# One attention kernel's first three head pairs: dividing by the row sums in the output projection, two value blocks to a PSUM bank, and every block of the first pair split

## The chip, the cores and the metric

The kernel is one program on one core of a Trainium2 chip. Its time is the device time in microseconds (us). The engines are PE (TensorE, the matrix engine; its sequencer also loads weights, PEld), DVE (VectorE), ACT (ScalarE), POOL (GpSimd) and SP (SyncE, whose queue starts the DMAs here).

## What is computed

Two decoder layers run over 1024 tokens of width 1024. In each, one projection feeds four mixers; their outputs are concatenated, projected and normalised, and a gated feed-forward follows. The part that matters is the softmax attention of two mixers, each of four heads:

```python
def one_block(args):
    q_blk, start = args
    s = jnp.einsum('bqhd,bkhd->bhqk', q_blk, k).astype(jnp.float32) * scale
    q_pos = start + jnp.arange(BLOCK)
    s = jnp.where(key_pos[None, :] <= q_pos[:, None], s, -jnp.inf)
    p = jax.nn.softmax(s, axis=-1).astype(v.dtype)
    return jnp.einsum('bhqk,bkhd->bqhd', p, v)
...
y = jnp.concatenate([y_a, y_b, y_c, y_d], axis=-1) @ w_out[l]
x = _layer_norm(DEEPNORM_ALPHA * x + y, ln1_g[l], ln1_b[l])
```

`y_b` (latent attention) is of this form; `y_c` (dilated windows, merged by their denominators) is computed by the kernel as one masked softmax too. Row sums divide the products of `p` and `v`; dividing before or after the product with `v` is the same.

## The kernel before

A layer's stages follow each other: the mixers without softmax, the projections for the others, `attention` (L1083, about 280 to 444 us in layer 0 and 1478 to 1642 in layer 1), `out_proj` (L1179), and the feed-forward.

**Attention** takes four head pairs, G[0] to G[3]: the first two are the dilated mixer's (mask `maskC`), the last two the latent one's (`maskB`). `attn` (L800) makes 16 rows of each pair: two heads (hh) by eight query blocks (i = 2*jp + e) of 128 tokens, with jp taken as (0,3) and then (1,2). A row goes through these steps: scores on PE into `sc`; DVE adds the mask and takes the minimum (L824); ACT takes exp in place and adds the row up (L828); DVE takes the sum's reciprocal (L830); POOL multiplies the row by it (L831); PE transposes the row's key blocks (L848) into a bank `pt`; ACT writes their rounded high part PH (L146) and DVE the rest, PL (L149). After both rows of a jp, PE adds up the value products into `pv` (L875), once with PH and once with PL. V holds a high and a low part in 128 columns, so a block's result has two 64-row parts that are added later. The table `FULL` lets some jp of a pair go undivided into high and low: G[0]'s jp 0 and 1 are copied whole (L854, by turns on ACT and DVE) and multiplied once, in fp32, by 64 columns of V.

ACT evacuates `pv` (L886, or L883) into `tmp` of 256 columns. For G[0] to G[2] two DMAs (L889) spill its parts to `yp` in memory; for G[3] DVE adds the parts into `Yb` (L884).

PE's order is written by hand: scores run three rows ahead (`ahead`), value sums follow two rows behind (VLAG), and projections of the next pair are filled in between (`self.jobs`). The other engines' orders come from a scheduler. PSUM pools are `mm` (3 banks: value sums and projections), `s` (2: scores) and `t` (3: transposes).

**out_proj** works on halves h of the tokens. `ysplit` brings eight operands: g = 0 and 3 come whole (L1192); for g = 1 and 2 the spilled parts are loaded (L1199) into one of two buffers, added on DVE (L1202), then cast on ACT and their rest taken on DVE (g = 1) or POOL (L149). The operand for f = 1 of g = 1 is `Yb`. PE's products are `po` (L124); DVE adds them to x (L1218).

The tags that matter in the rows below: `sc`, `pt`, `pv`, `po` are PSUM banks, `P` a row, `mn` its minimum, `rs` its sum, `yr` a loaded part and `yT` an operand of the projection.

## Time and profile before

| | us |
|---|---|
| median of 3 runs | 2399.78 |
| lowest and highest | 2398.84, 2403.02 |
| the profiled execution | 2400.5 |
| its span, first to last instruction | 2398.8 |

The mean granted TensorE clock of the profiled execution was 0.996 of full speed. Durations in the text are this execution's. Of an engine's busy time only what the others wait for counts, and that is read in the stretch where it happens: the rows of a stretch give the busy time of each engine in it, the waits give what ended an engine's idle time, and a timeline lists instructions with their start.

### The profile page before, as it was taken

What the parts mean: (1) busy time and instruction counts of PE and PEld (TensorE: products, weight loads), DVE (VectorE), ACT (ScalarE), POOL (GpSimd) and SP (SyncE); (2) the same over time, 40 slices, a digit from 0 to 9 for tenths busy, and PEclk for the clock granted to TensorE, in tenths of its full rate; (3) what the DMA queues carried; (4) which work ended last, traced back from release to release, by engine and by line L of the source; (5) the groups of instructions that cost most, each with busy time, mean ns of one, the idle gap of its engine ahead of it and who ended that gap; (6) DMA issues with size and microseconds to landing.
All of it is one profiled execution on the core that took longest, in us unless ns stands there. A gap on an engine that the chain in (4) does not pass through costs nothing.

```text
span 2398.8 us, 33440 instructions
## 1 busy us (share of the span) xinstructions
PE 2346.0 (98%) x11804; PEld 1971.7 (82%) x11804; DVE 1612.9 (67%) x2925; ACT 1004.8 (42%) x2004; POOL 1176.9 (49%) x1097
## 2 busy tenths in 40 slices
PE   9999999999999999999999999999999999999998
PEld 9789878777888888888897898788778888888886
DVE  7743588478765566767957435784787665667689
ACT  6323578334332323544343225783343323235442
POOL 2223525373545455767622244253735455547676
PEclk9999999999999999999999999999999999999999
DMA  4201112522332324653222110135213333345521
GB/s 169 65 29 43 31 37 83 186 110 70 115 114 87 113 99 170 216 189 101 93 66 64 36 37 31 38 87 188 110 62 114 116 102 107 108 164 208 189 97 70
DMA packets 91446, 246.81 MB, mean 103 GB/s; under 512 B 12096, under 2 KB 18560, under 8 KB 91280
## 3 DMA queue, kind: packets, MB, share of 16 engines
q1 hardware_dynamic: 91280, 244.68, 30.1%
q8 instruction: 94, 1.54, 0.3%
q14 instruction: 72, 0.59, 0.1%
HBM read 180.64 MB, written 64.52 MB: 102 GB/s over the span
## 4 chain that ended last, share of the span: by engine, by line
PE 82%; DVE 9%; issue 3%; ACT 3%; POOL 2%; DMA 1%; SPq 0%; POOLq 0%; ACTq 0%; DVEq 0%
PE gu L124 34%; PE dn L124 14%; PE zc L124 6%; PE po L124 5%; PE zvo L572 4%; PE zdq L524 3%; PE za L124 3%; PE zb L124 3%; PE pv L875 2%; PE sc L124 2%; PE dl L124 2%; DVE P L824 1%; PE pt L848 1%; DVE x L1136 1%; DVE PL L149 1%
## 5 line engine op out<-in xcount | busy, mean ns | idle before, releaser
L124 PE MATMUL gu<-T,fc 128*128 128x512 f32 x2640 | 625.9, 395 | 5.1 <-DVE T L1374 5.1
L124 PEld LDWEIGHTS gu<-T,fc 128*128 128x128 f32 x2640 | 496.7, 188 | 123.3 <-DVE T L1374 6.6
L1279 POOL TENSOR_TENSOR fc<-fw,fc 128x512 fp32r<-128x512 f32 x232 | 325.5, 1406 | 348.8 <-ACT fc L1278 341.9
L124 PE MATMUL dn<-dc,dc 128*128 128x512 f32 x1512 | 352.2, 395 | 0.0
L124 PEld LDWEIGHTS dn<-dc,dc 128*128 128x128 f32 x1512 | 283.7, 188 | 68.3 <-DVE dc L1279 1.0
L1278 ACT CAST fc<-fw 128x512 fp32r<-128x512 f32 x232 | 142.8, 620 | 349.5 <-PE gu L124 218.5
L124 PE MATMUL gu<-B,fc 128*128 128x512 f32 x1056 | 260.0, 396 | 0.0
L124 PEld LDWEIGHTS gu<-B,fc 128*128 128x128 f32 x1056 | 197.6, 188 | 46.6
L149 POOL TENSOR_TENSOR dc<-hr,dc 128x512 fp32r<-128x512 f32 x126 | 190.1, 1520 | 79.4 <-ACT dc L146 69.9
L1437 DVE TENSOR_TENSOR Ra<-Ra,gu 128x512 f32<-128x512 f32 x172 | 117.6, 684 | 118.6 <-PE gu L124 101.8
L831 POOL TENSOR_SCALAR P<-P,rs 128x256 f32<-128x256 f32 (+7 forms) x128 | 95.8, 752 | 152.4 <-DVE rs L830 94.9
L124 PE MATMUL po<-wh,yT 128*128 128x512 f32 x512 | 163.2, 397 | 0.6 <-DVE x L1218 0.6
L124 PE MATMUL zc<-wh,xT 128*128 128x384 f32 x512 | 134.1, 339 | 0.0
L1278 ACT CAST dc<-dr 128x512 fp32r<-128x512 f32 x108 | 67.0, 622 | 129.9 <-PE dn L124 75.1
L124 PEld LDWEIGHTS po<-wh,yT 128*128 128x128 f32 x512 | 95.8, 188 | 23.4 <-DVE x L1218 1.5
L124 PE MATMUL sc<-kst,q 128*128 128x512 f32 (+3 forms) x384 | 107.7, 375 | 6.7 <-DVE mn L824 6.6
L828 ACT ACTIVATE P<-P,mn 128x256 f32<-128x256 f32 (+7 forms) x128 | 99.9, 782 | 21.4 <-DVE mn L824 19.8
L1279 DVE TENSOR_TENSOR dc<-dr,dc 128x512 fp32r<-128x512 f32 x72 | 81.1, 1136 | 35.4 <-ACT dc L1278 35.4
L149 DVE TENSOR_TENSOR PL<-pt,PH 128x512 fp32r<-128x512 f32 (+3 forms) x176 | 95.6, 557 | 12.3 <-ACT PH L146 11.8
L140 POOL TENSOR_TENSOR wl<-raw,wh 128x768 fp32r<-128x768 f32 (+2 forms) x32 | 62.6, 1962 | 79.6 <-ACT wh L132 79.1
L124 PE MATMUL po<-wl,yT 128*128 128x512 f32 x256 | 100.7, 395 | 0.0
L848 PE MATMUL pt<-ident,P 128*128 128x128 f32 x576 | 89.2, 281 | 11.4 <-DVE PL L149 5.7
(393 smaller groups left out, 4896.3 us busy)
## 6 DMA issues: line engine op xcount, KB each, us to landing
fw<-in_wGU SPq DMA_DIRECT2D x88, 512.0 KB, 4.6
hr<-hs SPq DMA_DIRECT2D x142, 256.0 KB, 2.8
dr<-in_wD SPq DMA_DIRECT2D x44, 512.0 KB, 5.2
hs<-Ra SPq DMA_DIRECT2D x40, 512.0 KB, 2.9
hs<-Rb SPq DMA_DIRECT2D x22, 512.0 KB, 5.5
raw<-in_wO SPq DMA_DIRECT2D x16, 512.0 KB, 3.6
x<-x SPq DMA_DIRECT2D x16, 512.0 KB, 2.6
raw<-in_wC SPq DMA_DIRECT2D x16, 384.0 KB, 3.0
```

What stands on the lines that cost most here:

```text
L124: self.nc.tensor.matmul(out, lhsT=a, rhs=b, start=first and j == 0, stop=last and j == n - 1)
L140: (eng or nc.gpsimd).tensor_sub(lo[:, :n], raw[:, :n], f32(hi[:, :n]))
L149: (lo_eng or nc.vector).tensor_sub(lo, src, f32(hi))
L524: step(lambda: nc.tensor.matmul(pz, lhsT=a, rhs=b_, start=n == 0, stop=n == 23))
L572: nc.tensor.matmul(box["p"], lhsT=a, rhs=b_, start=j == 0, stop=j == 23)
L828: nc.scalar.activation(P[:, 0:nk], P[:, 0:nk], AF.Exp, scale=-1.0, bias=m, accum_out=rs[:, 0:1])
L831: nc.gpsimd.tensor_scalar(out=P[:, 0:nk], in0=P[:, 0:nk], scalar1=rs[:, 1:2], scalar2=1.0, op0=ALU.mult, op1=ALU.mult)
L848: nc.tensor.transpose(pt[:, b * 128:(b + 1) * 128], P[:, (b0 + b) * 128:(b0 + b + 1) * 128], self.ident)
L875: nc.tensor.matmul(pv[0:m, c0:256], lhsT=v(b), rhs=Pt[b // 4][:, b % 4, c0:256], start=b == 0 and x == 0, stop=b == nb - 1 and x == len(pa ...
L1278: nc.scalar.copy(dst[:, 0:512], src)
L1279: lo_eng.tensor_sub(dst[:, 512:1024], src, f32(dst[:, 0:512]))
L1437: tt = lambda o, a, b, op: v.tensor_tensor(out=o, in0=a, in1=b, op=op)
```

## The change

In G[0] to G[2], exp adds each row's sum into a column of a tile `sums` (128 x 16), and neither reciprocal nor multiplication follows. When a pair is through, `turn_sums` takes the reciprocal of the whole tile, turns it on PE, copies it on ACT and writes it to `yr` in memory. In `out_proj` two DMAs load these factors, each row spread over 64 partitions, into `rb`, and POOL multiplies the added spilled parts by them. G[3] still divides its rows. FULL is now empty, so all blocks of G[0] are split. And the two jp that follow each other (0 and 3, 1 and 2) put their sums into the halves of one bank, which is evacuated once, 512 columns at a time, and spilled by half as many DMAs.

```diff
@@ -34,7 +34,7 @@
 LATE_Y = 6
 SEQ, VLAG = "svt", 2
 AHEADS = (3, 3, 3, 3)
-FULL = [("AV",) * n + ("",) * (4 - n) for n in (2, 0, 0, 0)]
+FULL = [("AV",) * n + ("",) * (4 - n) for n in (0, 0, 0, 0)]
 NLAG, MAN = 0, {mybir.EngineType.PE}
 PPS = ("E", "B", "B", "B")
 NP = NF // 2
@@ -802,7 +802,7 @@
         nc = self.nc
 
         rows = [(G, jp, hh, 2 * jp + e) for G in groups for two in ((0, 3), (1, 2)) for hh in range(2) for e in range(2) for jp in two]
-        P_, PHL, norms = {}, {}, []
+        P_, PHL, norms, open_pv = {}, {}, [], [None]
 
         def scores(n):
             G, jp, hh, i = rows[n]
@@ -824,6 +824,11 @@
                 nc.vector.tensor_tensor_reduce(out=P[:, k0:k1], in0=sp[:, 0:k1 - k0], in1=mask[:, m0:m0 + k1 - k0], scale=-scale,
                                                scalar=mn[:, ch - 1:ch] if ch else 3.0e38, op0=ALU.add, op1=ALU.min, accum_out=mn[:, ch:ch + 1])
             m = mn[:, nch - 1:nch]
+            if "sums" in G:
+
+                c = hh * 8 + i
+                nc.scalar.activation(P[:, 0:nk], P[:, 0:nk], AF.Exp, scale=-1.0, bias=m, accum_out=G["sums"][:, c:c + 1])
+                return
             rs = self.sm("rs", 2)
             nc.scalar.activation(P[:, 0:nk], P[:, 0:nk], AF.Exp, scale=-1.0, bias=m, accum_out=rs[:, 0:1])
             def norm():
@@ -860,7 +865,15 @@
             V = G["V"]
             full = G["full"][jp]
             nb = 2 * jp + 2
-            pv = self.psum("pv", "mm")
+
+            both = not any(G["full"])
+            if both:
+                second = jp >= 2
+                if not second:
+                    open_pv[0] = self.psum("pv", "mm")
+                pv = open_pv[0][:, 256 * second:256 * second + 256]
+            else:
+                pv = self.psum("pv", "mm")
             pairs = PHL.pop((id(G), jp, hh))
             if "heads" in G:
                 v = lambda b: V[b // 2][:, b % 2, G["heads"] + hh, :]
@@ -874,15 +887,24 @@
                 for x, Pt in enumerate(pairs):
                     nc.tensor.matmul(pv[0:m, c0:256], lhsT=v(b), rhs=Pt[b // 4][:, b % 4, c0:256],
                                      start=b == 0 and x == 0, stop=b == nb - 1 and x == len(pairs) - 1)
+            if both:
+                if not second:
+                    return
+                pv, tmp = open_pv[0], self.t2("tmp")
+                blocks = lambda x: x.rearrange("p (j n) -> p j n", n=256)
+                if jp == 3:
+                    at = lambda x: blocks(x)[:, 0:4:3, :]
+                else:
+                    at = lambda x: blocks(x)[:, 1:3, :]
+                if "Y" in G:
+                    nc.scalar.copy(tmp[0:64, :], pv[0:64, :])
+                    nc.vector.tensor_tensor(out=at(G["Y"][64 * hh:64 * hh + 64, :]), in0=blocks(tmp[0:64, :]), in1=blocks(pv[64:128, :]), op=ALU.add)
+                    return
+                nc.scalar.copy(tmp, pv)
+                for part in range(2):
+                    nc.sync.dma_start(at(G["spill"][part][64 * hh:64 * hh + 64, :]), blocks(tmp[64 * part:64 * part + 64, :]))
+                return
             tmp = self.t2("tmp", 256)
-            if "Y" in G:
-                y = G["Y"][64 * hh:64 * hh + 64, jp * 256:(jp + 1) * 256]
-                if full:
-                    nc.scalar.copy(y, pv[0:64, 0:256])
-                else:
-                    nc.scalar.copy(tmp[0:64, :], pv[0:64, 0:256])
-                    nc.vector.tensor_tensor(out=y, in0=tmp[0:64, :], in1=pv[64:128, 0:256], op=ALU.add)
-                return
             nc.scalar.copy(tmp[0:m, :], pv[0:m, 0:256])
             for part in range(2):
                 dst = G["spill"][part][64 * hh:64 * hh + 64, jp * 256:(jp + 1) * 256]
@@ -1093,17 +1115,33 @@
                     zjobs.pop(0)()
         box = {}
 
+        def sums(g):
+            G[g]["sums"] = self.sp.tile([128, 16], F32, name=self.nm("sums"), tag="sums", bufs=2)
+
+        def turn_sums(g):
+
+            t = G[g]["sums"]
+            nc.vector.reciprocal(t, t)
+            pt = self.psum("prs", "t")
+            nc.tensor.transpose(pt[0:16, 0:128], t, self.ident)
+            r = self.t2("rsT", 128)
+            nc.scalar.copy(r[0:16, :], pt[0:16, 0:128])
+            nc.sync.dma_start(io["yr"][l, g], r[0:16, :])
+
         def start0():
+            sums(0)
             G[0].update(mask=self.mask, spill=io["yp"][l, 0])
             self.jobs = zjobs + self.prep_c_jobs(zc[1], G[1])
 
         def start1():
+            sums(1)
             G[1].update(mask=G[0]["mask"], spill=io["yp"][l, 1])
             w = box["w"] = self.b_weights(l)
 
             def st():
                 bb["qk"] = self.qk_tiles("E", G[0]["qk"][2])
             self.jobs = self.b_vqr_jobs(ct, w, bb) + [st] + self.b_qk_jobs(0, ct, w, bb, "qk")
+            self.jobs.insert(4, lambda: turn_sums(0))
 
         def start2():
             m = self.u("maskB")
@@ -1111,10 +1149,13 @@
             box["Yb"] = self.u("Yb", F32, "A")
             bb["qk1"] = self.qk_tiles("A", G[1]["qk"][2])
             G[2].update(heads=0, mask=m, spill=io["yp"][l, 2], qk=bb["qk"], V=bb["V"], R=bb["R"], QR=bb["QR"][0])
+            sums(2)
             self.jobs = self.b_qk_jobs(1, ct, box["w"], bb, "qk1")
+            self.jobs.insert(2, lambda: turn_sums(1))
 
         def start3():
             G[3].update(heads=2, mask=G[2]["mask"], Y=box["Yb"], qk=bb["qk1"], V=bb["V"], R=bb["R"], QR=bb["QR"][1])
+            self.jobs = [lambda: None, lambda: None, lambda: turn_sums(2)]
 
         for g, f in zip(G, (start0, start1, start2, start3)):
             g["start"] = f
@@ -1198,8 +1239,13 @@
                         raw = self.uw("yr", F32, "r")
                         nc.sync.dma_start(raw[:, 0:1024].rearrange("p (a n) -> p a n", a=2),
                                           io["yp"][l, f if g == 2 else 2][:, :, h * 512:h * 512 + 512].rearrange("a p n -> p a n"))
+                        gg = f if g == 2 else 2
+                        rb = self.t2("rb")
+                        for hh in range(2):
+                            nc.sync.dma_start(rb[hh * 64:hh * 64 + 64, :], io["yr"][l, gg].rearrange("(a t) p -> a (t p)", a=2)[hh:hh + 1, h * 512:(h + 1) * 512].to_broadcast([64, 512]))
                         y[f] = raw[:, 0:512]
                         nc.vector.tensor_tensor(out=y[f], in0=y[f], in1=raw[:, 512:1024], op=ALU.add)
+                        nc.gpsimd.tensor_tensor(out=y[f], in0=y[f], in1=rb, op=ALU.mult)
                 for f in range(2):
                     k = g * 2 + f
                     t = self.u("yT", F32R, "y" if g == 1 and h == 1 else "A").rearrange("p (a n) -> p a n", a=2)
@@ -1771,6 +1817,7 @@
     io["crow"] = nc.dram_tensor("crow", (L, 8, 512), F32, kind="Internal").ap()
     io["ys"] = nc.dram_tensor("ys", (L, 2, 2, 128, 1024), F32, kind="Internal").ap()
     io["yp"] = nc.dram_tensor("yp", (L, 3, 2, 128, 1024), F32, kind="Internal").ap()
+    io["yr"] = nc.dram_tensor("yr", (L, 3, 16, 128), F32, kind="Internal").ap()
     io["x1"] = nc.dram_tensor("x1", (L, S, D), F32, kind="Internal").ap()
     io["hs"] = nc.dram_tensor("hs", (L, NP, 4, 128, S), F32, kind="Internal").ap()
     io["xs"] = nc.dram_tensor("xs", (S, D), F32, kind="Internal").ap()
```

Three places show what becomes of the instruction order. Names end in a number of the tile, and `ISA` rows are the masked minimum of L824.

On DVE, early in the first pair of layer 0, before (rs are the row sums, PT the undivided transposed blocks, ra a rotation of the next pair's keys):

```order
L830 RECIPROCAL rs_2883<-rs_2883 128x1
L824 ISA P_2893,mn_2894<-sc_2899,maskC_2686,mn_2894 128x512
L824 ISA mn_2894 128x1
L854 COPY PT_2920<-pt_2921 128x128
L824 ISA P_2924,mn_2925<-sc_2926,maskC_2686 128x128
L824 ISA mn_2925 128x1
L223 TENSOR_TENSOR ra_2914<-zc_2850,cs_169 128x256
L224 TENSOR_TENSOR ra_2914<-zc_2850,sn_170 128x4x32
L225 TENSOR_TENSOR ra_2914<-zc_2850,sn_170 128x4x32
L830 RECIPROCAL rs_2903<-rs_2903 128x1
```

and after:

```order
L824 ISA P_2885,mn_2886<-sc_2891,maskC_2686,mn_2886 128x512
L824 ISA mn_2886 128x1
L824 ISA P_2915,mn_2916<-sc_2917,maskC_2686 128x128
L824 ISA mn_2916 128x1
L223 TENSOR_TENSOR ra_2903<-zc_2848,cs_169 128x256
L224 TENSOR_TENSOR ra_2903<-zc_2848,sn_170 128x4x32
L225 TENSOR_TENSOR ra_2903<-zc_2848,sn_170 128x4x32
L149 TENSOR_TENSOR PL_2910<-pt_2911,PH_2909 128x128
```

The two reciprocals are gone, and the copy to PT has become a subtraction that needs PH from ACT and that stands behind the next row's minimum and the rotation.

On PE, where the last pair's value sums hand over to the output projection in layer 0, before (a line of dots stands for rows of the same kind; po ending in 5234 is the first output tile, 5262 the second):

```order
L875 MATMUL pv_5131<-PH_5085,V_3331 128x256
L124 MATMUL po_5234<-wh_5169,yT_5197 128x512
...
L124 MATMUL po_5234<-wh_5176,yT_5206 128x512
...
L875 MATMUL pv_5131<-PL_5087,V_3331 128x256
...
L875 MATMUL pv_5131<-PL_5088,V_3333 128x128
L124 MATMUL po_5262<-wh_5169,yT_5197 128x512
```

and after (5071, 5099 and 5127 are the first three output tiles):

```order
L888 MATMUL pv_4948<-PL_4892,V_3288 128x128
L124 MATMUL po_5071<-wh_4994,yT_5022 128x512
...
L124 MATMUL po_5099<-wh_4994,yT_5022 128x512
...
L888 MATMUL pv_4948<-PH_4914,V_3287 128x256
...
L888 MATMUL pv_4948<-PL_4917,V_3289 128x128
L124 MATMUL po_5127<-wh_4994,yT_5022 128x512
```

Before, the products of a third operand (yT ending in 5206, made of the first spilled part) stand between the value products, and the second output tile opens after the last of them. After, two output tiles are opened ahead of the second half of the shared bank, with two operands, and the third tile is opened behind it; there are three banks in that pool.

On SP, the queue of DMAs around the same place, before (x are the tokens' tiles, yr 5203, 5212 and 5215 the three spilled loads):

```order
L1192 DMA yr_5195<-ys 128x1024
L1199 DMA yr_5203<-yp 128x2x512
L1199 DMA yr_5212<-yp 128x2x512
L1199 DMA yr_5215<-yp 128x2x512
L1214 DMA x_5232<-in_x 128x1024
L1192 DMA yr_5224<-ys 128x1024
L1214 DMA x_5260<-in_x 128x1024
```

and after (rb are the factors):

```order
L1240 DMA yr_5028<-yp 128x2x512
L1240 DMA yr_5041<-yp 128x2x512
L1260 DMA x_5069<-in_x 128x1024
L1245 DMA rb_5030<-yr 64x512 x2
L1245 DMA rb_5043<-yr 64x512 x2
L1245 DMA rb_5050<-yr 64x512 x2
L1260 DMA x_5097<-in_x 128x1024
L1260 DMA x_5125<-in_x 128x1024
L1260 DMA x_5153<-in_x 128x1024
L1245 DMA rb_5191<-yr 64x512
L1240 DMA yr_5048<-yp 128x2x512
```

The third spilled load has moved behind four x tiles and seven factor loads, and the first factors stand behind the first x tile.

## Rows read from the trace of the kernel before

**Rows 1.** The page, busy time of each engine over the whole span.

```profile
PE 2346.0 (98%) x11804; PEld 1971.7 (82%) x11804; DVE 1612.9 (67%) x2925; ACT 1004.8 (42%) x2004; POOL 1176.9 (49%) x1097
```

**Rows 2.** Windows: stretch, length, busy time of PE, PEld, DVE, ACT, POOL, clock, DMA.

```profile
280.00:325.00 45.00, 38.82 (x253) 31.36 (x252) 37.89 (x114) 35.85 (x82) 19.43 (x26) 0.96 0.09 26
325.00:400.00 75.00, 70.93 (x488) 63.16 (x488) 62.44 (x187) 60.99 (x146) 26.55 (x38) 1.00 0.18 48
400.00:444.00 44.00, 38.75 (x262) 33.53 (x261) 34.14 (x103) 32.59 (x78) 26.31 (x27) 1.00 0.32 96
444.00:490.00 46.00, 45.68 (x198) 36.61 (x197) 9.12 (x14) 10.63 (x15) 20.14 (x13) 1.00 0.67 244
...
286.00:290.00 4.00, 3.67 (x15) 2.39 (x12) 3.28 (x7) 3.71 (x8) 2.63 (x5) 0.57 0.00 0
318.00:322.00 4.00, 1.73 (x10) 0.96 (x8) 3.94 (x10) 2.99 (x7) 0.48 (x1) 1.00 0.00 0
```

**Rows 3.** Waits, 275 to 445 us: total, times, longest, all in us.

```profile
POOL P L831 <- DVE rs L830: 45.9, 31, 4.4
...
DVE rs L830 <- ACT P L828: 5.8, 12, 1.2
...
PE sc L124 <- DVE mn L824: 3.6, 9, 1.5
...
PE pt L848 <- DVE PL L149: 2.8, 4, 1.0
...
PE pt L848 <- POOL P L831: 2.4, 2, 1.6
...
PE pv L875 <- DVE q L797: 1.6, 2, 1.2
```

**Rows 4.** Timeline around 284 us: start, duration, engine, instruction, idle before.

```profile
283.44 0.69 DVE L149 TENSOR_TENSOR PL<-pt,PH 128x512 fp32r<-128x512 f32 x1
...
284.27 0.41 PE L848 MATMUL pt<-ident,P 128*128 128x128 f32 x2 [1.58 <-POOL P L831]
```

**Rows 5.** Timeline of PE around 307 us.

```profile
306.77 1.73 PE L875 MATMUL pv<-PT,zcv 128*64 128x256 f32 x8
308.43 0.55 PE L848 MATMUL pt<-ident,P 128*128 128x128 f32 x3
```

**Rows 6.** Groups by line and shape, 280 to 444 us: busy us, mean ns.

```profile
L149 DVE TENSOR_TENSOR PL<-pt,PH 128x512 fp32r<-128x512 f32 x46 | 31.4, 686 | 5.8 <-ACT PH L146 5.7
...
L830 DVE RECIPROCAL rs<-rs 128x1 f32<-128x1 f32 x61 | 9.5, 157 | 5.5 <-ACT P L828 4.9
...
L797 DVE TENSOR_TENSOR q<-pqb,q 64x512 fp32r<-64x512 f32 x8 | 5.5, 686 | 0.3 <-ACT q L796 0.2
L796 ACT CAST q<-pqb 64x512 fp32r<-64x512 f32 x8 | 4.7, 581 | 1.4 <-PE pqb L124 1.1 <-DVE q L797 0.2
...
L149 DVE TENSOR_TENSOR PL<-pt,PH 128x128 fp32r<-128x128 f32 x14 | 4.0, 284 | 0.1
```

**Rows 7.** Groups by line, shapes together, 280 to 444 us.

```profile
L854 DVE COPY PT<-pt 128x128 f32<-128x128 f32 (+1 forms) x4 | 1.7, 422 | 0.2 <-PE pt L848 0.2
```

**Rows 8.** Timeline of the handover to the output projection, layer 0.

```profile
441.92 0.28 PE L875 MATMUL pv<-PL,V 128*128 128x256 f32 x1
...
442.04 0.22 PE L875 MATMUL pv<-PH,V 128*128 128x128 f32 x1
...
442.42 0.37 ACT L883 COPY tmp<-pv 64x256 f32<-64x256 f32 x1 [0.90 <-PE pv L875]
```

**Rows 9.** Tiles yT and yr, 400 to 500 us: duration ns min/median/max.

```profile
L149 POOL TENSOR_TENSOR yT<-yr,yT x12: 1292/1298/1321, 415.1 to 474.4; 128x512 fp32r<-128x512 f32 x12
L149 DVE TENSOR_TENSOR yT<-yr,yT x2: 681/686/692, 420.4 to 465.5; 128x512 fp32r<-128x512 f32 x2
...
DMA to landing us min/median/max: 3.1/3.8/9.6
```

## The prediction

> **What bounds the kernel now.** I read the engines' totals first: TensorE (PE) is busy 98% of the span [rows 1], so time can leave only where PE idles, waits or runs at its lower clock, or where it is given less work. The instruction order differs only between the start of attention and the end of the output projection, twice (two layers), so I then read layer 0's stretches [rows 2]. Between 280 and 444 us PE idles 6.2 us of the first 45 (the first pair), 4.1 of the next 75 (second and most of the third), 5.2 of the last 44 (mostly the fourth): 15.5 us. In 444 to 490, the rest of the projection's first half of columns, it idles 0.32 us. So the prize is some 10 us a layer in the changed pairs, and the projection has nothing to gain and a full cover to lose.
>
> Third, what ends PE's waits there [rows 3]: scores wait 3.6 us for the mask's minimum on VectorE (DVE), transposes 2.8 us for DVE's low halves PL and 2.4 us for the normalise on GpSimd (POOL), value sums 1.6 us for DVE. The long list of POOL waiting for DVE (45.9 us) is idle time of an engine that is not late. The single wait that names POOL has to be looked at: at 284.27 PE is said to have waited 1.58 us for POOL [rows 4], but no POOL record ends there; DVE's PL ends at 284.13 and frees the transposes' bank. So these waits are mostly DVE's, in a stretch where DVE is busy 37.9 of 45 us and ScalarE (ACT) 35.9 [rows 2]. Removing POOL's multiplication doesn't by itself remove them.
>
> **The change part by part** (all per layer, times two at the end).
>
> (1) The two blocks of 2 and the two of 4 key blocks in the first pair that used one fp32 product per key block use two split products. Eight fp32 instructions run from 306.77 to 308.43, 1.66 us [rows 5]; they are one block of four key blocks (a product in fp32 shows as two instructions), and the split products step by 0.12 us (441.92 to 442.04) [rows 8], half that for 128 columns by their width: six of 0.12 and two of 0.06 are 0.83. That saves 0.83 for each block of four, 0.47 for each of two: 2.6 us of PE work. But this is the pair in which PE idles 6.2 us behind DVE and ACT, so most of the saving turns into longer waits. I take -0.8; bounds 0 and -2.6.
>
> (2) Three transposes of the sums, each a bank, an ACT copy and one DVE reciprocal: +0.3 (0 to +0.6), two or three PE steps of about 0.1 us each.
>
> (3) DVE loses 48 reciprocals of 157 ns, 7.5 us [rows 6], and with them most of the 5.8 us that it stood at the queue's head waiting for ACT's exp [rows 3]; what is queued behind is the next row's mask and the PL that PE waits for. It gains eight subtractions of 284 to 686 ns [rows 6], mean 0.485, for four copies of 422 ns [rows 7]: +2.2 us, all in the first pair, which nearly cancels that pair's 16 reciprocals (2.5 us). So the first pair gets little, pairs two and three get 5 us less DVE work against about 5 us of idle PE. I take half, -2.5; bounds 0 and -7 (all the first three pairs' DVE waits of rows 3).
>
> (4) Two blocks share one of the three banks of the pool that also holds projections, so fewer banks are asked for and value sums should no longer wait for one: 1.6 us [rows 3], of which I take -1.2 (0 to -1.6). ACT evacuates 512 columns at once; a 64x512 copy-like cast takes 581 ns against 370 for each of two 256-column copies [rows 6, 8], off the path.
>
> (5) At the end of the last pair this turns round. Before, the last value block ended at 442.4 and PE went straight into the projection, while ACT's copy (0.37 us, 442.42) ran beside it [rows 8]; the third bank had been given back earlier. After, PE does the first two output tiles' ready products, then finishes the shared bank, and the third output tile needs that very bank: PE waits for a 512-column copy (0.58 us by the 64x512 cast) and a DVE add (0.69 us by the 64x512 subtraction) [rows 6], +0.15 for the handings-on: +1.4 (0 to +1.6). Nothing else is ready on PE's hand-written order.
>
> (6) In the projection, each spilled pair now gets a POOL multiplication between DVE's add and ACT's cast: 128x512 on POOL takes 1.30 us by the subtraction of that shape [rows 9]. Its factors come by two broadcast DMAs each, queued on SP behind the first x tile; I take them as landed by then. In the first half of the tokens two load buffers exist, so the third load waits until the first pair's low half is subtracted on DVE, now behind the 64x512 add. The value sums end 0.7 us later than 442.4 (three more ready products stand ahead of them), copy, add and subtraction take 0.58, 0.69 and 0.69, handing on and issue about 0.5: some 445.6. Landing 3.8 [rows 9], add 0.69, product 1.30, cast 0.62 (an estimate for 128x512 from the 64x512's 0.58) give 452.0. PE resumes at some 444.6 and first wants that operand 33 products of 0.23 us (198 in 45.7 us) [rows 2] later: 452.2. Just in time. In the second half the chain is three products, 3.9 us, longer; counted the same way from its third load it comes about 1 us late. I take +1.0 (0 to +3.9). What hides it is the 0.2 us of margin and PE's other products; if this cover is gone every further microsecond is paid.
>
> The row for the subtraction shows POOL at 1298 ns and DVE at 686 ns for one shape [rows 9], 0.61 us more for each link. The Trainium skill, "GPSIMD Engine Reference", section 4.1 (Engine selection), says to put elementwise work of two inputs on VectorE, GpSimd being about twice as slow; the trace agrees (1.9 times). By that rule the six multiplications stand on the wrong engine; with them on DVE term 6 would be 0 and the time 2 us lower. No run here shows that placement.
>
> Edits with one answer: the sums' small DMAs, half as many spill DMAs and the 48 normalisations gone from POOL free queues that nobody waits for.
>
> Sum: -0.8 + 0.3 - 2.5 - 1.2 + 1.4 + 1.0 = -1.8 a layer, -3.6 in all. The profiled execution took 2400.5 us (span 2398.8, 1.7 around it), 0.7 above the median of the runs: 2396.9, by the median's measure 2396.2. **Forecast 2396 us.**
>
> **Rivals.**
>
> R1, the large gain: POOL's product and the reciprocals were the row's latency, and three quarters of the 10.3 us idle of the first two stretches goes (-7.7); PE's clock, granted at 0.57 from 286 to 290 [rows 2] after the idle before it, stays at the upper of its levels (2.4 GHz, not 1.2), another -1.7. With -0.8, +0.3 and +1.4: -8.5 a layer, 2400.5 - 17.0 - 0.7 = 2383. For it: DVE is the releaser of most of these waits. Against: DVE and ACT keep 84% and 80% of the first pair, and from 318 to 322 PE idled more (1.73 of 4 us busy) with the clock at 1.00 [rows 2], so the clock is not simply bought with less idle time.
>
> R2, the change doesn't do what it says for the time: the removed links were never late (rows 4), and the scheduler refills DVE so that terms 3 and 4 are zero. Then -0.8 + 0.3 + 1.4 + 1.0 = +1.9 a layer, or +2.7 without term 1: 2403.6 to 2405.2, say 2404.
>
> R3, slower: the third spill load lands late. Landings range to 9.6 us [rows 9], and DMA is busy 67% in 444 to 490 [rows 2] where this load now falls. From 4.0 us on, PE waits; at 9.6 it waits 5.6 us a layer more: -1.8 + 5.6 = +3.8, 2400.5 + 7.6 - 0.7 = 2407. For it: the wide x loads and weights are queued around it. Against: the median landing is 3.8.
>
> **How the numbers follow.** About 0.2% (4.8 us) is what a measurement of this kernel can tell from no change: faster is below 2395.0, slower above 2404.6. Forecast 0.42, spread from 2391 to 2400 by its bounds: 0.17 faster, 0.25 same. R1 0.24, all faster. R2 0.20: 0.11 same, 0.09 slower. R3 0.14: 0.04 same, 0.10 slower. In all 0.41, 0.40, 0.19. The range 2384 to 2406 leaves out the lower half of R1 (0.12) and the upper half of R3 (0.07). Both signs hold much chance; the forecast's own range is 2391 to 2400.
>
> **What the profile after would show.** Terms 1 to 4: PE's idle time from the start of attention to the fourth pair's rows falls from 10.3 us to about 6; waits of transposes that name POOL are gone there, those for PL stay in the first pair (if they vanish, R1; if nothing falls, R2). Term 5: one wait of the third output tile for a DVE add into Yb, 1.2 to 1.6 us, once a layer. Term 6: waits of output products for operands whose chain goes through the POOL multiplication, under 1.5 us a layer; many of 3 us or more is R3. Wrong altogether would be a new idle time of PE elsewhere: ffn or the mixers, whose order is the same, and a clock that falls in other places.

## The result: 1.3% slower, and the profile after

The changed kernel takes 2432.85 us (median of 4 runs, 2431.88 to 2434.36), the kernel before 2401.09 beside it: a ratio of 1.0133, interval 1.0116 to 1.0151. The forecast was 2396 us, with a range that ended at 2406. In the profiled execution the span is 2430.2 us, 31.4 more than before, with a mean granted clock of 0.992.

TensorE's total hardly moved, so the time is idle time and lower clock. The page's engine totals of the changed kernel (before: [rows 1]):

```profile
PE 2352.9 (97%) x11810; PEld 1977.9 (81%) x11810; DVE 1604.1 (66%) x2835; ACT 1007.2 (41%) x1986; POOL 1124.7 (46%) x1013
```

The same four stretches of layer 0 as in [rows 2], same columns, then three short ones:

```profile
280.00:325.00 45.00, 36.45 (x243) 31.60 (x242) 36.38 (x99) 34.85 (x79) 5.87 (x8) 0.92 0.12 31
325.00:400.00 75.00, 70.38 (x479) 61.95 (x478) 60.34 (x161) 60.01 (x137) 4.91 (x8) 1.00 0.18 47
400.00:444.00 44.00, 37.64 (x256) 33.02 (x255) 32.33 (x97) 32.58 (x75) 24.48 (x26) 0.96 0.26 73
444.00:490.00 46.00, 39.16 (x161) 30.64 (x161) 10.87 (x16) 8.37 (x15) 18.15 (x15) 0.93 0.74 245
...
458.00:460.00 2.00, 0.00 (x0) 0.00 (x0) 0.69 (x1) 0.00 (x0) 0.18 (x1) 1.00 1.03 260
...
462.00:464.00 2.00, 2.00 (x5) 1.62 (x6) 0.00 (x0) 1.14 (x2) 2.00 (x2) 0.50 1.01 309
464.00:466.00 2.00, 2.00 (x6) 1.54 (x5) 0.00 (x0) 0.00 (x0) 1.56 (x2) 0.50 1.04 420
```

POOL fell from 19.4 and 26.6 to 5.9 and 4.9 us in the first two stretches; PE gained nothing from it: its idle time there rose from 10.3 to 13.2 us, where about 6 was forecast. The stretch with nothing to gain, 444 to 490, now has 6.8 us of idle PE in place of 0.32, and after an idle gap PE is busy all the time at a granted 0.50, the lower level (1.2 of 2.4 GHz).

For all runs I cut a layer at three events: first score product, last score product, last product of the output projection (layer 0 before: 273.8, 432.2, 535.2 us). Between the first two lies attention, between the last two the projection. Differences to the kernel before, from one profiled execution each, which lies up to 4 us from its kernel's median (e3's 4.0 above, e13's 3.7 and e18's 3.4 below), so that a difference of two or three microseconds says little:

| kernel | median us | ratio, interval | attention, layers 0, 1 | projection, layers 0, 1 |
|---|---|---|---|---|
| before | 2401.09 | 1 | 158.4, 159.4 us | 103.0, 102.4 us |
| changed | 2432.85 | 1.0133, 1.0116 to 1.0151 | +5.2, +3.3 | +11.1, +12.3 |
| e1 no factors | 2428.93 | 1.0111, 1.0096 to 1.0126 | +5.7, +6.2 | +9.4, +10.9 |
| e2 split alone | 2406.11 | 1.0021, 1.0012 to 1.0030 | +3.5, +0.7 | +0.1, +0.8 |
| e3 shared banks alone | 2420.29 | 1.0076, 1.0059 to 1.0092 | +10.7, +4.1 | +6.1, +5.4 |
| e4 sums alone | 2410.78 | 1.0037, 1.0024 to 1.0050 | -4.1, -5.0 | +8.4, +10.5 |
| e5 as e3, last pair apart | 2407.82 | 1.0036, 1.0024 to 1.0048 | +2.3, +3.6 | 0.0, +0.5 |
| e6 changed, last pair apart | 2431.37 | 1.0129, 1.0115 to 1.0143 | +1.6, +3.8 | +13.7, +11.5 |
| e7 changed, products on DVE | 2426.68 | 1.0109, 1.0095 to 1.0123 | +3.1, +0.3 | +8.5, +12.5 |
| e8 sums in two pairs | 2403.76 | 1.0010, 1.0002 to 1.0019 | -1.1, -2.6 | +3.6, +3.4 |
| e9 changed, operand order | 2430.89 | 1.0127, 1.0113 to 1.0141 | +0.7, -0.8 | +10.6, +10.8 |
| e10 sums, operand order | 2421.04 | 1.0083, 1.0069 to 1.0097 | +1.2, -1.2 | +6.4, +7.9 |
| e11 changed, x filled | 2425.95 | 1.0108, 1.0094 to 1.0122 | +2.8, +0.6 | +12.0, +12.3 |
| e12 before, reciprocal on POOL | 2416.30 | 1.0064, 1.0050 to 1.0078 | +8.3, +9.0 | -0.1, +0.6 |
| e13 sums, loads ahead | 2394.41 | 0.9972, 0.9961 to 0.9983 | -3.8, -5.8 | +2.5, +0.7 |
| e14 changed, loads ahead | 2400.21 | 1.0000, 0.9991 to 1.0009 | -0.1, -2.0 | +2.8, +2.2 |
| e15 changed, no x | 2414.92 | 1.0056, 1.0039 to 1.0073 | +2.7, +3.4 | +3.5, +7.5 |
| e16 before, no x | 2400.02 | 1.0001, 0.9991 to 1.0010 | +0.8, -0.5 | -0.4, +0.1 |
| e17 before, loads ahead | 2392.89 | 0.9960, 0.9947 to 0.9974 | -0.1, -1.7 | -1.1, -0.1 |
| e18 as e13, products on DVE | 2392.16 | 0.9961, 0.9949 to 0.9974 | -4.4, -6.1 | +1.2, -0.2 |

Three quarters of the loss (23.4 of 31.4 us) lies in the projection. Its waits in layer 0, from the changed kernel's timeline of PE:

```profile
449.68 0.50 PE L124 MATMUL po<-wh,yT 128*128 128x512 f32 x1 [1.40 <-DVE Yb L901]
461.78 0.80 PE L124 MATMUL po<-wh,yT 128*128 128x512 f32 x1 [4.19 <-ACT yT L146]
```

The first is the shared bank's wait of the fifth term. The second is the operand of the third load, forecast for 452.2. Its chain is read backwards, engine by engine. SP's queue of the changed kernel (start, time until the last of the group, count):

```profile
416.63 9.97 SPq L1240 DMA_DIRECT2D yr<-yp  x2
443.29 0.35 SPq L1260 DMA_DIRECT2D x<-in_x  x1
443.68 4.14 SPq L1245 DMA_DIRECT2D rb<-yr  x6
448.21 1.30 SPq L1260 DMA_DIRECT2D x<-in_x  x3
...
451.47 0.38 SPq L1240 DMA_DIRECT2D yr<-yp  x1
```

and the instructions between those loads, from the timelines of ACT, POOL and DVE in turn:

```profile
448.33 0.58 ACT L900 COPY tmp<-pv 64x512 f32<-64x512 f32 x1 [4.53 <-PE pv L888]
449.68 0.62 ACT L146 CAST yT<-yr 128x512 fp32r<-128x512 f32 x1 [0.77 <-DMA rb<-yr]
...
461.11 0.62 ACT L146 CAST yT<-yr 128x512 fp32r<-128x512 f32 x1 [9.56 <-POOL yr L1248]
```

```profile
448.38 2.52 POOL L1248 TENSOR_TENSOR yr<-yr,rb 128x512 f32<-128x512 f32 x2 [6.90 <-DMA rb<-yr]
...
459.82 1.26 POOL L1248 TENSOR_TENSOR yr<-yr,rb 128x512 f32<-128x512 f32 x1 [6.62 <-DMA rb<-yr]
```

```profile
450.33 1.12 DVE L149 TENSOR_TENSOR yT<-yr,yT 128x512 fp32r<-128x512 f32 x1 [0.70 <-ACT yT L146]
...
459.05 0.69 DVE L1247 TENSOR_TENSOR yr<-yr 128x512 f32<-128x512 f32 x1 [7.00 <-DMA yr<-yp]
```

The first factors are issued from 443.68 and reach POOL at 448.38. Only then follow product, ACT's cast and DVE's low half (450.33); it empties the buffer that the third load needs, issued at 451.47. Its data is added at 459.05, 7.6 us after the issue, with the DMA engines full (share 1.03 at 458 to 460). Product, cast, and PE goes on at 461.78. ACT's copy of the last bank also stands at its queue's head from 443.8 to 448.33, and no cast is done before it. In SP's queue of the kernel before all three loads had been started long before (the last row is those of the second half of the tokens):

```profile
413.59 7.87 SPq L1199 DMA_DIRECT2D yr<-yp  x3
436.13 0.34 SPq L1214 DMA_DIRECT2D x<-in_x  x1
442.40 0.33 SPq L1192 DMA_DIRECT2D yr<-ys  x1
...
454.45 12.17 SPq L1199 DMA_DIRECT2D yr<-yp  x3
```

### The profile page after: what moved, and what is told of

The parts are those of the page before. It is cut to its first block, busy times and chain, and to the rows that moved or that the text cites. A ratio compares the mean times of both kernels' runs of the same rounds, so it can differ in the third digit from the quotient of the medians.

```text
span 2430.2 us, 33056 instructions
## 1 busy us (share of the span) xinstructions
PE 2352.9 (97%) x11810; PEld 1977.9 (81%) x11810; DVE 1604.1 (66%) x2835; ACT 1007.2 (41%) x1986; POOL 1124.7 (46%) x1013
## 5 line engine op out<-in xcount | busy, mean ns | idle before, releaser
L124 PE MATMUL po<-wh,yT 128*128 128x512 f32 x512 | 167.4, 404 | 14.6 <-ACT yT L146 10.6
L149 DVE TENSOR_TENSOR PL<-pt,PH 128x512 fp32r<-128x512 f32 (+2 forms) x192 | 102.5, 552 | 17.4 <-ACT PH L146 16.4
L853 PE MATMUL pt<-ident,P 128*128 128x128 f32 x576 | 90.5, 281 | 17.2 <-DVE PL L149 13.2
L798 POOL CAST q<-q 64x512 fp32r<-64x512 f32 x32 | 19.6, 612 | 184.7 <-ACT q L796 183.8
L146 ACT CAST PH<-pt 128x512 fp32r<-128x512 f32 (+2 forms) x192 | 86.6, 480 | 22.0 <-PE pt L853 21.2
```

Source lines behind the costliest of these rows:

```text
L124: self.nc.tensor.matmul(out, lhsT=a, rhs=b, start=first and j == 0, stop=last and j == n - 1)
L146: nc.scalar.copy(hi, src)
L149: (lo_eng or nc.vector).tensor_sub(lo, src, f32(hi))
L798: nc.gpsimd.tensor_copy(q1[hh][o, cols], f32(q1[hh][r, cols]))
L853: nc.tensor.transpose(pt[:, b * 128:(b + 1) * 128], P[:, (b0 + b) * 128:(b0 + b + 1) * 128], self.ident)
```

## The experiments

**Parts alone.** First each part of the change on the kernel before, or the change without one part.

e1, no factors:

```diff
-                        rb = self.t2("rb")
...
-                        nc.gpsimd.tensor_tensor(out=y[f], in0=y[f], in1=rb, op=ALU.mult)
```

> The changed kernel without the factor loads and the six multiplications in the output projection (leaves out the division of the first three pairs by their row sums; the sums are still formed, turned and written). Theory A: the loss sits in the projection's operand chain (factors late, third spilled load late, then the lower clock), about 10 us a layer; expected some 2412 us, 20 below the changed kernel, no wait of output products for the operand cast over 1 us, and no half clock in the 30 us after the last value sums. Rival B: the shared last bank delays the operands by itself, so the chain stays late without factors: 2426 or more.

It came 4 us below the changed kernel, as rival B had it: without any product 9.4 and 10.9 us of the projection's loss stay. So the products aren't the sole cause. One wait carries most of it (waits of PE, 444 to 535 us):

```profile
PE po L124 <- ACT yT L146: 5.7, 1, 5.7
```

Its operand is one that comes whole (`ys`): the load was started at 453.91, behind eight x tiles.

e2, the split alone:

```diff
-FULL = [("AV",) * n + ("",) * (4 - n) for n in (2, 0, 0, 0)]
+FULL = [("AV",) * n + ("",) * (4 - n) for n in (0, 0, 0, 0)]
```

> The kernel before with only the first pair's blocks all split. Theory A with my term 1: -0.8 to +2 us a layer, so 2398 to 2404. Rival C: the attention loss of the changed kernel (some 5 us in layer 0 and 3 in layer 1) comes from the split blocks, DVE and ACT being the bound there: 2407 to 2410, with more waits of transposes for DVE's low halves in the first pair.

5 us slower, between the two ranges. Over the run PE's busy time fell by 3.0 us (2346.0 to 2343.0) and its idle time rose by 7.2 (52.8 to 60.0). Between 310 and 325 the granted clock is 0.77 (before 1.00).

e3, shared banks alone, and e5, the same with the last pair's apart:

```diff
-            both = not any(G["full"])
+            both = not any(G["full"]) and "Y" not in G
```

> The kernel before with only the shared banks, in the second to the fourth pair (the first keeps its undivided blocks, which do not share). Theory A with my terms 4 and 5: about 0 to +1 us a layer, 2400 to 2403, with one wait of 1.2 to 1.6 us of the third output tile for the add into Yb. Rival B: +5 us a layer or more, 2411 and up, as the projection's third spilled load comes late behind the last bank.

> The kernel before with shared banks in the second and third pair only. Theory D (new): in the fourth pair the one late, doubled evacuation stands at the head of ACT's and DVE's queues, so the casts of the loaded parts, their load buffers and the loads behind them come late; without sharing there the projection costs what it did before, within 1 us a layer, and only the attention part of the second and third pair is left: 2403 to 2409. Rival E: it is the held bank in the projections' pool that costs, in every pair alike: 2411 or more.

The sharing costs 18 to 19 us, 10 to 12 of them by the last pair alone. In the projection of e3 PE waits, from 444 to 535 us:

```profile
PE po L124 <- DVE x L1242: 3.5, 1, 3.5
...
PE po L124 <- DVE Yb L895: 1.4, 1, 1.4
```

The 1.4 is the handover. The 3.5 is a bank that DVE's sum to x frees; DVE had stood 13.56 us at the sum of a spilled part of the second half, whose load was issued at 467.77 (before 454.45). Ahead of it stand late casts and buffers: the casts of the loaded operands are behind ACT's last copy, and the load of `ys` that was issued at 442.40 before is issued at 459.27. In pairs two and three (e5) sharing loses 2.3 and 3.6 us in attention, where a gain was forecast. PE's waits of e5 from 275 to 445 us, in the form of [rows 3]:

```profile
PE sc L124 <- DVE mn L824: 5.6, 10, 1.4
...
PE pv L882 <- DVE q L797: 1.7, 2, 1.2
```

The wait of the value sums, which sharing was to remove, is as long as before (1.6 us), and scores wait 2.0 us more for the mask's minimum.

e6, the changed kernel with the last pair's banks apart:

> The changed kernel with the last pair's blocks in banks of their own again. Theory D: the third output tile's wait of 1.4 us goes, and part of the fourth pair's waits; but casts still stand behind the last evacuation because the multiplications do: 2420 to 2426. Rival F (the factors alone make the chain late, as the runs without them hint little of): 2431 to 2434. Rival G (the last pair's bank is nearly all of it): under 2417.

No gain, as rival F had it. The last bank is enough to make the projection late, and so are the factors (e4); with both the loss is no sum.

e4, the sums alone (banks apart, FULL as before):

```diff
-            both = not any(G["full"])
+            both = False
```

> The changed kernel with the banks apart and the first pair's two blocks undivided again, so only the sums, their turning and the factors are left. Theory A: the projection loses 8 to 10 us a layer as in the changed kernel, attention gains up to 2.5 us a layer: 2412 to 2420. Rivals B and C (the loss is the bank's or the split's): 2396 to 2402.

This parts the change into its gain and its loss: attention is 4.1 and 5.0 us shorter, the projection 8.4 and 10.5 longer.

e8 keeps the sums in the first two pairs only, whose factors are ready early:

> Sums and factors for the first two pairs only; the third pair divides its rows as before; banks apart, the first pair's two blocks undivided; the factors lie in a pool that the projection's second set of weights takes later, and are loaded ahead of the x tiles. Theory D: attention keeps two thirds of what the run with sums only gained (some 5 us a layer, so -3.5), and the first operand's cast, its buffer and the third load are early again, so the projection loses 0 to 3 us a layer instead of 8: 2392 to 2400. Rival F (any factor in the projection costs the 8 us a layer): 2408 or more.

Above the forecast range: gain and loss both shrink and nearly cancel, and some 2.5 us of loss stay.

**What the late operands are late for.** e7, `nc.vector` for `nc.gpsimd` in the product:

> The changed kernel with the six multiplications on DVE instead of POOL. By my term 6 and its rule (1.30 against 0.69 us a link) 2 us less: 2430 to 2431. Theory D: the chain waits for loads and for the last evacuation, not for the product's engine, so 2431 to 2434, no change.

6 us faster than the changed kernel, outside both ranges, and still 26 slower than before.

e9 and e10 take the operands in another order, the late ones last:

```diff
-            for g in range(4):
+            for g in (0, 3, 1, 2):
...
-                self.dense_tok(pz, TY, t, W, 512, 0, 512)
+                self.dense_tok(pz, TY, t, W, 512, 0, 512, ks=(0, 1, 6, 7, 2, 3, 4, 5))
```

> The changed kernel with the projection's operands taken in another order: the two that are loaded whole and need no factor (g = 3) come second, ahead of the three with factors; weights and products follow. Nothing else moves. Theory D: PE then has 12 products a tile ready while casts stand behind the last evacuation, their buffers are freed early and their loads come before the x tiles; the projection's loss falls from 11 to 12 us a layer to 2 to 5, the attention's 3 to 5 stays: 2409 to 2419. Rival H (the loss is spread over the projection and not in that chain): 2428 or more.

> Sums and factors for three pairs, banks apart, the first pair's blocks undivided (as in the run with sums only), the factors in the later weights' pool, and the operands in the new order. Theory D: attention gains 4 to 5 us a layer as in the run with sums only, the projection loses 1 to 3: 2392 to 2397, ahead of both kernels. Rival H: the projection still loses 8 or more, 2408 to 2412.

Both missed; e9 came as rival H had it. In e9 the largest wait of layer 0's first half fell to 2.1 us, but the operands of the second half were late in their turn, and the stretch from there to the next layer's attention took 6.9 us longer. An order of use doesn't mend an order of loading.

e11 fills the x tiles instead of loading them:

```diff
-                    nc.sync.dma_start(X[t], xsrc[t * 128:(t + 1) * 128, :])
+                    nc.vector.memset(X[t], 0.0)
```

> The changed kernel with the eight 512 KB loads of x in each output projection replaced by a fill with zeros on DVE (leaves the residual out of the result); casts and products stay behind the last evacuation. Theory D, first half (the casts' place alone makes the loss): the projection still loses 8 or more of its 11 to 12 us a layer, total 2424 or more. Second half (late loads are slow because they share the DMA engines with the x tiles and the factors stand behind x in SP's queue): third load lands in under 5 us instead of 7, the projection loses 3 to 6, total 2409 to 2420.

Not decisive: eight fills of 0.91 us stood ahead of the last `Yb` sum in DVE's queue, and PE waited 5.93 us for that instead. e15 leaves out load and fill, e16 is its control:

```diff
-                    nc.sync.dma_start(X[t], xsrc[t * 128:(t + 1) * 128, :])
...
-                nc.vector.scalar_tensor_tensor(out=xs, in0=xs, scalar=ALPHA, in1=pz, op0=ALU.mult, op1=ALU.add)
+                nc.vector.tensor_copy(xs, pz)
```

> The changed kernel without loads of x and without a fill: DVE copies the projection's result instead of adding it to x, so the residual of the first normalisation is left out. No x tile shares the DMA engines or stands ahead of a load. If the traffic of the x tiles is what makes the loads late, the projection's loss falls to 3 to 6 us a layer, against e16: 14 to 20 us slower than e16 in place of 32. If it falls by less than 2 us a layer, that traffic is not the cause.

> The kernel before with the same part left out, the control for e15. Its loads were early anyway and DVE's copy takes about as long as the sum, so every theory expects the time of the kernel before, 2396 to 2402 us.

e15 is 14.9 us above e16, in place of 31.8: about half of the loss goes with the x tiles' traffic and their place in the queue. The chain behind the third load is the same there, and its two ends show what went, SP's issue and DVE's sum of the data:

```profile
447.89 0.37 SPq L1240 DMA_DIRECT2D yr<-yp  x1
```

```profile
452.19 0.69 DVE L1247 TENSOR_TENSOR yr<-yr 128x512 f32<-128x512 f32 x1 [3.67 <-DMA yr<-yp]
```

That is 4.3 us in place of 7.6, and PE no longer waits for a late operand in either layer: of the 4.19 us nothing is left. What stays of the projection's loss, 3.5 and 7.5 us, is mostly the bank's 1.40, a wait of 2.56 and 3.25 us for the normalised x, and in layer 1 the lower clock.

**Loads ahead of the x tiles.** e13 on the kernel of e4, e14 on the changed kernel, e17 on the kernel before (which has no `rb`):

```diff
-                        raw = self.uw("yr", F32, "r")
+                        raw = self.u("yr", F32, "v")
...
-                        rb = self.t2("rb")
+                        rb = self.u("rb", F32, "v")[:, 0:512]
```

> The kernel of e4 (reciprocals applied in the projection, banks apart, first pair as before), with the loaded parts and the factors in buffers of the pool that later holds the second half of the weights: all three spilled loads, their factors and the loads of the operands that come whole are started ahead of the first x tile, instead of the third spilled load behind three x tiles. If late loads cause the projection's loss (8.4 and 10.5 us in e4), at most 3 us a layer of it stay, and with e4's gain in attention (4 to 5 us a layer) the time is 2391 to 2398 us. If the longer chain behind each load causes it (the GpSimd product, the casts), 6 to 8 us a layer stay, as in e10, and the time is 2403 to 2410.

> The changed kernel with the same buffers, so that every load of the first half of the tokens is started ahead of the x tiles. Late loads as the whole cause: the projection falls by some 9 us a layer, to 2413 to 2418 us. Late loads beside casts that stand behind the evacuation of the last shared bank (e3 lost 5.4 to 6.1 us there without any factor): 5 to 6 us a layer stay, 2420 to 2424. Neither: 2429 to 2434.

> The kernel before with the spilled loads in buffers of their own, so that all loads of the first half of the tokens start ahead of the x tiles. If late loads are a loss that the change made, the kernel before has none to give back (PE idles 2 to 2.6 us a layer in its projection): 2397 to 2402 us. If early loads are a gain of their own, it falls as far as e13 stands below it, to 2390 to 2395.

e13 came as the theory of late loads had it. e14 gave back more than either theory allowed, 32.6 us: 8.3 and 10.1 a layer in the projection, and 5.3 a layer in attention, which I hadn't expected. SP's queue in e14:

```profile
434.31 0.38 SPq L1240 DMA_DIRECT2D yr<-yp  x1
434.74 1.64 SPq L1245 DMA_DIRECT2D rb<-yr  x2
436.43 0.59 SPq L1240 DMA_DIRECT2D yr<-yp  x1
438.75 1.08 SPq L1245 DMA_DIRECT2D rb<-yr  x2
439.88 0.59 SPq L1240 DMA_DIRECT2D yr<-yp  x1
440.57 1.08 SPq L1245 DMA_DIRECT2D rb<-yr  x2
441.75 2.49 SPq L1260 DMA_DIRECT2D x<-in_x  x4
```

The third load and the first factors start earlier than in the changed kernel (439.88 against 451.47, 434.74 against 443.68), the first two loads later (434.31 and 436.43, against 416.63 for the first). The DMA table, 434 to 490 us (count, size, median from issue to landing), shows landings about as slow as in the changed kernel, where x tiles took 7.2 us and four spilled loads 7.5:

```profile
x<-in_x SPq DMA_DIRECT2D x8, 512.0 KB, 8.3
yr<-yp SPq DMA_DIRECT2D x6, 512.0 KB, 6.3
```

So a slow landing is hidden here by a start ahead of the wait. PE's waits for operands over the whole run, of the changed kernel and of e14 (busy, mean ns, idle before and its releasers):

```profile
L124 PE MATMUL po<-wh,yT 128*128 128x512 f32 x512 | 167.4, 404 | 14.6 <-ACT yT L146 10.6 <-DVE Yb L901 2.8 <-DVE x L1264 1.3
```

```profile
L124 PE MATMUL po<-wh,yT 128*128 128x512 f32 x512 | 163.4, 397 | 6.3 <-ACT yT L146 2.9 <-DVE Yb L901 2.8 <-DVE x L1264 0.6
```

Part of attention's loss has a row too. In the changed kernel DVE, inside the last pair, stands at the sum of a spilled part until its load lands, with rows' minima and PL queued behind it:

```profile
420.62 0.69 DVE L1247 TENSOR_TENSOR yr<-yr 128x512 f32<-128x512 f32 x1 [2.04 <-DMA yr<-yp]
```

PE is busy 7.61 us of 420 to 430 there, at a clock of 0.83. In e14 these sums start at 444.3, behind attention, and in 420 to 430 PE is busy 9.37 at 1.00. (Before, DVE stood there too, 1.49 us for POOL.) These buffers thus change two things at once, the loads' place in the queue and the place of the sums on DVE, and no run parts them. Of the 5.3 us that e14 has back in layer 0's attention the clock's loss is 3.4: 1.7 here, and 1.7 behind a wait at 320 us that is as long in e14 (2.40 us, in the changed kernel 2.35).

e17 brought the surprise: the kernel before gains 7.7 us by the same buffers, so they are a gain of their own. Its loads are not all earlier, as SP's queue shows:

```profile
434.47 1.40 SPq L1199 DMA_DIRECT2D yr<-yp  x3
435.98 3.77 SPq L1214 DMA_DIRECT2D x<-in_x  x4
439.80 2.20 SPq L1199 DMA_DIRECT2D yr<-yp  x3
```

Those of the first half start later than before (434.47 against 413.59), those of the second half earlier (439.80 against 454.45). Against e17 the whole change still costs 7.3 us (2400.21 against 2392.89, two sets of runs; by the ratios 0.0040, some 10 us) and the sums alone 1.5. Of the change's 31.8 us, then, 22 to 24 go with these buffers, and 7 to 10 are its own.

e18, the products of e13 on DVE:

> The kernel of e13 with the six products by the factors on DVE in place of GpSimd. The products stand behind the attention there, where DVE is idle most of the time (a row of e13: busy 3 to 7 us of 10), and each link is 0.6 us shorter; e13's projection still takes 2.5 and 0.7 us more than that of the kernel before. If that rest is the products' chain: 2 to 4 us faster than e13, 2390 to 2393. If it is something else, the time of e13 within 1 us.

2.2 us below e13, with intervals that overlap, and level with e17. e13, e17 and e18 are all faster than both kernels; the gain is that of the buffers, and none of the change's parts adds to it that can be measured.

**Row latency or DVE's queue.** e12, on the kernel before, takes the reciprocal from DVE and gives it to POOL, as a power of -1:

```diff
-                nc.vector.reciprocal(rs[:, 1:2], rs[:, 0:1])
+                nc.gpsimd.tensor_tensor(out=rs[:, 1:2], in0=rs[:, 0:1], in1=self.mone[:, 0:1], op=ALU.pow)
```

> The kernel before with each row's reciprocal taken on POOL (a power of -1 of the sum) instead of DVE; nothing else is changed, so the output projection keeps its operands. If what sums only gained in attention came from DVE's queue (64 small instructions of 157 ns that wait there for ACT's sum), it comes here too: attention 2 to 4 us a layer shorter, the projection as before, 2392 to 2397. Rival: it came from the row's latency through POOL, which here grows by one more POOL instruction: 2400 to 2406.

Its group of the 64 reciprocals between 275 and 445 us:

```profile
L832 POOL TENSOR_TENSOR rs<-rs,mone 128x1 f32<-128x1 f32 x64 | 35.5, 557 | 50.7 <-ACT P L830 47.6 <-DVE V L149 2.5
```

DVE is freed of 64 reciprocals of 157 ns [rows 6], each row's chain grows by 0.4 us, and attention takes 8.3 and 9.0 us longer, beyond the rival's range. So taking the reciprocals from DVE is no gain by itself. That the row's chain is what counts isn't shown: POOL's queue, too, now waits for the sum that the reciprocal needs (47.6 us of its idle time in the row).

## Why the prediction was wrong, step by step

**What bounds the kernel.** The reading that the projection had nothing to gain and a full cover to lose was right, and it is what happened. Then I priced the loss of that cover at 1 us.

**Term 1, -0.8, bounds 0 and -2.6.** Wrong sign: e2 lost 3.5 and 0.7 us in attention. The bounds excluded a loss because less PE work was counted as no worse. PE did have less to do, 1.5 us a layer by its busy time, but its idle time rose by 3.6. In layer 0 the lower clock adds to it: 0.77 over the 15 us from 310 is a loss of 3.4 us. The transposes are not where the waits grew. Their group before, then in e2:

```profile
L848 PE MATMUL pt<-ident,P 128*128 128x128 f32 x576 | 89.2, 281 | 11.4 <-DVE PL L149 5.7 <-POOL P L831 4.9 <-DVE kst L790 0.3
```

```profile
L848 PE MATMUL pt<-ident,P 128*128 128x128 f32 x576 | 89.5, 281 | 12.0 <-DVE PL L149 11.5
```

They wait 12.0 us in place of 11.4, and what stood under POOL stands under DVE's PL. The rest is spread over waits for DVE of 1 to 2 us. That the plain copies, now pairs of ACT and DVE, are the reason is argued, not shown.

**Term 2, +0.3.** No run measured it by itself. The changed kernel has a wait for the turned sums' copy in each layer, 2.35 us at 320 and 1.33 in layer 1; what holds the copy up is ahead of it in ACT's queue, the load of a constant (`selr`). The rows of PE and ACT:

```profile
320.17 0.58 PE L853 MATMUL pt<-ident,P 128*128 128x128 f32 x2 [2.35 <-ACT rsT L1128]
```

```profile
318.44 1.04 ACT L1065 CAST selq<-selr 128x1024 fp32r<-128x1024 f32 x1 [2.25 <-DMA selr<-in_c_selq]
```

PE stood around there before as well [rows 2, 318 to 322], with 1.33 us as its longest wait, so what the copy adds isn't known.

**Term 3, -2.5.** Right in sign: -4.1 and -5.0 in e4, within the bound of -7. Of that PE's idle time is -1.9 and -1.3, less than the term. Most of the rest goes with the clock, which the term had no place for: before, it is at the lower level once in layer 0's attention (0.57 from 286 to 290) and twice in layer 1's, 1.7 us of loss each; in this execution of e4, its fastest, never. So the size may in part be luck of one execution. As forecast, no transpose waits for POOL any more in the first three pairs; over the run transposes wait 10.3 us in e4, against 11.4 before.

**Term 4, -1.2, bounds 0 and -1.6.** Wrong sign: e5 lost 2.3 and 3.6 us in attention. The wait that it was to remove is still there (1.7 us in e5, 1.6 before), so it was not a wait that sharing banks ends. I saw one evacuation in place of two; it comes later and is longer, and stands at the head of ACT's queue. That this is the reason for the loss was argued, not shown.

**Term 5, +1.4.** The wait was 1.40 us, once a layer, as worked out. What was missed is behind it: "nothing else is ready on PE's hand-written order" was asked of PE alone. On ACT, the casts of loaded operands are queued behind that copy, and their buffers and loads behind the casts. e3 against e5: 12.5 us by the medians, 9.6 by the ratios.

**Term 6, +1.0, bounds 0 and +3.9. This is the step that failed most.** Alone, in e4, it measured 8.4 and 10.5 us a layer. Attention ends some 5 us later in the changed kernel, so the working is held against it from the end of the last value sums (forecast 443.1, measured 448.3):

| from the end of the value sums | forecast | measured |
|---|---|---|
| third load issued | 2.5 us | 3.2 |
| its data summed, from the issue | 3.8 | 7.6 |
| operand ready | 8.9 | 13.5 |
| PE wants it | 9.1 | 9.3 |

So issue and PE's need were nearly right, and the landing failed: taken at the median of 3.8 [rows 9], it was 7.6 us here, 7.7 in layer 1, and PE waited 4.19 and 3.98 us. In e4, with the banks apart, it was 6.0 and the wait 3.28; in e15, without x tiles, 4.3 and no wait. The range of the landing, up to 9.6, stood in the same row, and x tiles are queued right there. The factors, "as landed by then", arrived at 448.38, with the end of the value sums, and cost little. In the second half operands came late by 0.93 and 1.49 us at the most, near the 1 us of the sum. One part of the loss was no term at all, the lower clock after the gap: over the run PE's idle time grew by 24.5 us and the time lost to the lower level by 8.8 (each stretch's length times what its granted clock lacks to 1), while the split took some 3 us of PE's work away.

The Trainium skill, "GPSIMD Engine Reference", section 4.1 (Engine selection), would put the products on VectorE, worth 2 us by my sum. e7 gained 6, and e18 2.2 with intervals that overlap: both go the rule's way, and it is not the main matter.

**Rivals.** R3 was the mechanism that came: waits of 3 us or more for operands whose load is late. Its rule, waiting from a landing of 4.0 us on, gives 3.6 us for the 7.6 that came, and 4.19 was measured. It took one load as late and left all else in place; with the bank's wait, the later operands and the clock the projection loses 11 to 12 us a layer. R1's gain in attention shows in e4 and e13, with less time at the lower clock as it had said, and is paid for.

**What stays open.** Why the buffers bring the kernel before 7.7 us: in the profiled execution it is 6.3, and attention, projection and the stretch between the layers show 4.5 of that, in no one place. And how the change's own rest of 7 to 10 us divides: the projection of e14 takes 3.9 and 2.3 us more than that of e17; attention is level, a gain by the sums (e13 stands 3.7 and 4.1 us below e17) and a loss of that size by split and banks (e14 against e13, 3.7 and 3.8). These are single executions, e13's 3.7 us below its median and e17's 1.3 above; by the medians e13 stands 1.5 us above e17.

## What to carry to other kernels

Price a moved load by what shares the DMA engines while it lands, not by the median of other loads, and by its start: what is queued ahead of it, which buffer it needs, what must run before that buffer is free, and whose queue each of these steps stands in. A wait at a handover is not done with when PE resumes; follow what stood behind the waiting instruction on the other engines. And when a change rearranges loads, try the loads' order by itself, on the kernel before too: here it was worth more than the change.

## What the runs showed of the hardware that was not expected

- The same wait is followed by the lower clock in one run and not in another: at 320 us PE waits 2.35 us in the changed kernel, with a granted clock of 0.79 from 318 to 326, and 2.40 us in e14, with 1.00. And the clock fell where no gap was long: 0.83 in the changed kernel's 420 to 430, with 0.94 us as PE's longest gap there.
- On POOL a power over 128x1 takes 557 ns, where DVE's reciprocal of the same shape takes 157 [rows 6].
- A 512 KB load took 7.6 us from issue to use beside the x tiles and 4.3 without them (e15). Started ahead of the wait, as in e14 (median landing 6.3), it left PE 1.44 us of waiting for an operand in layer 0's first half in place of 4.19.
